# Weight casts queued behind the norm of the first token block, and a latent transposed one unit later

## Chip, cores and metric

One core of a Trainium2 chip. The metric is the device time of one execution in microseconds; of several runs the median counts.

## The reference, cut to what matters

The kernel computes one block of an encoder: x of 256 tokens by 2048 features goes through a gated FFN, a mixer (latent attention beside gated linear attention) and a second gated FFN, each behind a norm with scale and shift.

```python
mod = (jax.nn.silu(c) @ w_ada[i] + b_ada[i]).reshape(B, N_MOD, D)
h = _rms_norm(x, g_ffn1[i]) * (1.0 + sc1) + sh1
x = x + 0.5 * ga1 * _swiglu(h, w1_a[i], w3_a[i], w2_a[i])
h = _rms_norm(x, g_mix[i]) * (1.0 + sc2) + sh2
(q_lat, kv_lat, k_rope_raw, gq, gk, gv, g_lr, g_out, gate_a, gate_b) = _split_cols(h @ w_in[i], IN_SPLITS)
...
x = x + ga2 * (merged @ w_out[i])
h = _rms_norm(x, g_ffn2[i]) * (1.0 + sc3) + sh3
x = x + 0.5 * ga3 * _swiglu(h, w1_b[i], w3_b[i], w2_b[i])
```

The change touches the second and the third `_rms_norm` with the first weights that follow each, and the norm of `kv_lat`.

## The kernel before

**Tiling.** The 256 tokens are two blocks (tb 0 and 1) of 128. x lies in `x_sb`, tokens on partitions. For a product the activations are transposed to `hT` (features on partitions, 16 tiles k of 128), and the weights stream in as units of 1 MB (four k tiles by 512 columns) into one of three `raw` buffers.

**Three products for one.** Each fp32 operand is split in a high part (a cast to fp32r) and a low part (the value less the high part). `split_raw` makes two pieces of 1024 columns of each unit: ScalarE (ACT) casts raw to `wh` (L125), VectorE (DVE) subtracts to `wl` (L126). Six buffers each hold them. `mm3` issues three matmuls, L137 (wh), L140 (wl) and L141 (low activations).

**The end of a stage.** `add_product` makes the last 512 columns (n = 3) in two halves: block 0's matmuls of the last three units first, then `mid`, then block 1's. `mid` calls `resid` for block 0: DVE scales (L405) and adds to x_sb (L407), ACT squares with a sum (L291), `finish_rstd` forms the variance on DVE (L307) and GpSimd (POOL) raises it to -0.5 (L309). Then `then(tb)` from `next_hT` makes hT of the next stage in four groups of four k tiles: `xn_T` scales on ACT (L341) and transposes on PE (L344); `mod_T` applies scale and shift, half on DVE (L356) and half on ACT (L359), casts the high part on ACT (L364) and subtracts the low part on DVE (L365). Block 1 goes the same way after its own matmuls.

**After it.** In the mixer the first product is the kv latent, `lat` (four units, block 0 first for the first three); in the second FFN it is `a1`. After `lat`, `latent` normalizes it (L787 on ACT, L793 `ln` on DVE) and returns `finish`, called `kv_done`, which transposes `ln` on PE (L804), scales (L809) and splits it to ckvh and ckvl (L695, L696). Eight units of `w_qc` follow, in two accumulators, `qc0` and `qc1`, one for each block; `qc1` takes the buffer of `lat`. ckv is first used in `mla_pair(0)`, after the eight units.

**The order.** The kernel is written in program order, and a scheduler puts the instructions on each engine when the program is built: of those that it takes to be ready, the one written first goes first; `high_priority` lifts a block, `keep_in_program_order` pins an instruction. On the chip each engine then goes through its list in that order and waits where an operand or buffer is not there. `issue_after(ins)` adds an edge in this order alone: the instructions of its block on the engine of `ins` are queued behind `ins`. SyncE (SP) issues the weight loads, in order, each as a raw buffer comes free.

Of the kernel before, what the change touches and what calls it, by code (L numbers as in the profile page):

```python
# [10 lines left out]
F32 = mybir.dt.float32  # L11
# [3 lines left out]
ALU = mybir.AluOpType  # L15
# [4 lines left out]
D = 2048  # L20
# [43 lines left out]
def layer_kernel(ctx: ExitStack, tc: tile.TileContext, a: dict):  # L64
    nc = tc.nc
    PE, ACT, DVE, POOL, SP = nc.tensor, nc.scalar, nc.vector, nc.gpsimd, nc.sync
# [45 lines left out]

    last_cast = [None]

    def split_raw(raw, src_cols, n):

        res = []
        per = max(1, (src_cols // n) // 2)
        k = 0
        while k * n < src_cols:  # L120
            w = min(per * n, src_cols - k * n)
            wh = hl.tile([P, 1024], F32R, tag="wh", name="wh")
            wl = hl.tile([P, 1024], F32R, tag="wl", name="wl")
            src = raw[:, k * n:k * n + w]
            last_cast[0] = ACT.copy(wh[:, :w], src)  # L125
            DVE.tensor_tensor(wl[:, :w], src, wh[:, :w].bitcast(F32), op=ALU.subtract)  # L126
            for q in range(w // n):
                res.append((wh[:, q * n:(q + 1) * n], wl[:, q * n:(q + 1) * n]))
            k += w // n
        return res  # L130

    def unit_parts(ap, nkt, n):

        return split_raw(load_unit(ap, nkt * n), nkt * n, n)

    def mm3(out, xh, xl, wh, wl, start, stop, pin=False):
        m = PE.matmul(out, xh, wh, start=start, stop=False)  # L137
        if pin:
            tc.keep_in_program_order(m)
        PE.matmul(out, xh, wl, start=False, stop=False)  # L140
        PE.matmul(out, xl, wh, start=False, stop=stop)  # L141
# [142 lines left out]
    ss_t = const.tile([P, TB, 4], F32, name="ss_t")  # L284
# [11 lines left out]
    def early_rstd():  # L296
# [3 lines left out]
        DVE.tensor_scalar(t[:, TB:2 * TB], t[:, 0:TB], scalar1=1.0 / D, scalar2=EPS, op0=ALU.mult, op1=ALU.add)  # L300
        return POOL.tensor_tensor(rs_t, t[:, TB:2 * TB], mhalf[:, 0:TB], op=ALU.pow)

    def finish_rstd(tb):
        t = wk.tile([P, 16], F32, tag="st", name="ssum", bufs=4)
        DVE.tensor_reduce(t[:, 0:1], ss_t[:, tb, 0:3], axis=AX.X, op=ALU.add)
        DVE.tensor_scalar(t[:, 1:2], t[:, 0:1], scalar1=1.0 / D, scalar2=EPS, op0=ALU.mult, op1=ALU.add)
        DVE.tensor_scalar(t[:, 2:3], ss_t[:, tb, 3:4], scalar1=1.0 / D, scalar2=t[:, 1:2],  # L307
                          op0=ALU.mult, op1=ALU.add)
        POOL.tensor_tensor(rs_t[:, tb:tb + 1], t[:, 2:3], mhalf[:, 0:1], op=ALU.pow)  # L309

    def new_hT_tb(tb):
        return (hTp.tile([P, KT, P], F32R, tag=f"hTh{tb}", name="hTh"),
                hTp.tile([P, KT, P], F32R, tag=f"hTl{tb}", name="hTl"))

    def next_hT(i):

        hT = []

        def then(tb):
            hT.append(new_hT_tb(tb))  # L320
            for kg in range(4):
                with tc.high_priority() if kg == 0 else nullcontext():
                    norm_T(hT, i, tb, kg * 4, 4)
        return hT, then

    def new_hT():
# [5 lines left out]
    def norm_T(hT, i, tb, k0, nk):  # L332

        mod_T(hT, i, tb, k0, nk, xn_T(tb, k0, nk))

    last_xn = [None]

    def xn_T(tb, k0, nk, in_order=False):
        w = nk * P
        xn = wkA("xn")  # L340
        last_xn[0] = ACT.mul(xn[:, :w], x_sb[:, tb, k0 * P:k0 * P + w], rs_t[:, tb:tb + 1])  # L341
        ps = bank("xT")
        for k in range(nk):
            t = PE.transpose(ps[:, k * P:(k + 1) * P], xn[:, k * P:(k + 1) * P], ident)  # L344
            if in_order:
                tc.keep_in_program_order(t)
        return ps

    def mod_T(hT, i, tb, k0, nk, ps, early=False):
        w = nk * P  # L350
        hf = wkB("hf")
        for k in range(nk):
            kt = k0 + k
            o, s_ = hf[:, k * P:(k + 1) * P], ps[:, k * P:(k + 1) * P]
            if k % 2 == 0 and not early:
                DVE.tensor_scalar(o, s_, scalar1=ab[i][:, kt:kt + 1],  # L356
                                  scalar2=ab[i][:, KT + kt:KT + kt + 1], op0=ALU.mult, op1=ALU.add)
            else:
                ACT.activation(o, s_, AF.Identity, scale=ab[i][:, kt:kt + 1],  # L359
                               bias=ab[i][:, KT + kt:KT + kt + 1])  # L360
        hi = hT[tb][0][:, k0:k0 + nk, :]
        lo = hT[tb][1][:, k0:k0 + nk, :]
        hv = hf[:, :w].rearrange("p (k t) -> p k t", k=nk)
        ACT.copy(hi, hv)  # L364
        DVE.tensor_tensor(lo, hv, hi.bitcast(F32), op=ALU.subtract)  # L365
# [34 lines left out]
    def resid_ops(acc, g, n, tbs, tail):  # L400
        nt = len(tbs)
        t = wkA("res")
        tv = t[:, :nt * 512].rearrange("p (t n) -> p t n", t=nt)
        av = acc[tbs[0]].unsqueeze(1) if nt == 1 else acc
        DVE.tensor_tensor(tv, av, g(n).unsqueeze(1).broadcast_to([P, nt, 512]), op=ALU.mult)  # L405
        xv = x_sb[:, tbs[0]:tbs[0] + nt, n * 512:(n + 1) * 512]
        DVE.tensor_tensor(xv, xv, tv, op=ALU.add)  # L407
        for tb in tbs if tail else ():
            sumsq_chunk(tb, n)
            if n == 3:  # L410
                finish_rstd(tb)
# [45 lines left out]
    with tc.tile_pool(name="f1", bufs=1, reuse_waits="tile") as f1, \  # L457
# [185 lines left out]
        for r, grp in enumerate(raws_of):  # L643
            known = set(ada_done)
            fill(int(target(r)) - (n_all - len(ada_q)))
            if r == 0:
                h_tiles(known)
            raw = load_unit(a["w_open"][r], pool=lambda: ramp_raw(True if grp[0][0] == 0 else None))
            if grp[0][0] == 0:
                weights = [raw[:, q * 512:(q + 1) * 512] for q in range(4)]  # L650
            else:
                if grp[0][0] == 1 and len(pacc) < 4:
                    pacc.append([bank("pacc2"), bank("pacc3")])
                    free_slots.insert(0, 3)
                weights = split_raw(raw, 2048, 512)
                do_todo(r)
            if r == 3:
                high_tiles(0, 1, hfs[0])
            low_tiles()
            h_tiles(known)  # L660
            assert not h_rows or all(k < h_rows[0][0] for _, _, _, k in grp), (r, grp, h_rows)
            if any(k0 <= k < k0 + n for k0, n, _ in lows for _, _, _, k in grp):
                low_tiles()
            for q, ((gi, c, wi, k), w) in enumerate(zip(grp, weights)):
                product(r, gi, (c, wi), k, w)
                if gi == 0 and x_blocks and q < 3:
                    with tc.issue_after(first_hf[0].ins):
                        x_blocks.pop(0)()
            if not h_rows and x_again and r >= X_AGAIN:
                x_again.pop(0)()  # L670
            if grp[-1][0] == last_group and (c, wi) not in FRONT[-1] and 3 in free_slots:
                free_slots.remove(3)
# [3 lines left out]
        with tc.issue_after(last_cast[0].ins):  # L676
# [7 lines left out]
        gTs, flush = ffn_up(a["w1_a"], a["w3_a"], chunks, f1r, xs)  # L684
        mod_cols(1, 0, 16, C_GMX)
        hT, then = next_hT(1)
        ffn_down(a["w2_a"], list(chunks), gTs, flush, g_row, True, after=lambda n: fill(1000 if n == 2 else 0),
                 then=then)
# [19 lines left out]
    with tc.tile_pool(name="mx", bufs=1, reuse_waits="tile") as mx:  # L708
# [4 lines left out]
        with tc.tile_pool(name="mla", bufs=1, reuse_waits="tile") as ml:  # L713
# [6 lines left out]
            for tb in range(TB):  # L720
                DVE.tensor_scalar(ang[:, tb * 32:(tb + 1) * 32], rows[:, 128:160],
                                  scalar1=posf[:, tb:tb + 1], scalar2=None, op0=ALU.mult)
# [96 lines left out]

            accs = [acc_tile("qc0"), acc_tile("qc1")]  # L820
            for u in range(8):
                if u == 2:
                    kv_done()
                for j, (wh, wl) in enumerate(unit_parts(a["w_qc"][u], 2, 592)):
                    k = u * 2 + j
                    for tb in range(TB):
                        xh, xl = xs(k, tb)
                        for e, (c0, c1) in enumerate(((0, 320), (320, 592))):
                            mm3(accs[tb][:, e, :c1 - c0], xh, xl, wh[:, c0:c1], wl[:, c0:c1],
                                start=(k == 0), stop=(k == KT - 1))  # L830
# [25 lines left out]
            for tb in range(TB):  # L856
                DVE.tensor_scalar(kr[:, tb, 0, :], accs[tb][:, 0, 256:320], scalar1=krs[:, tb:tb + 1],
                                  scalar2=None, op0=ALU.mult)
# [157 lines left out]
        with tc.tile_pool(name="late", bufs=1, reuse_waits="tile") as lt, ExitStack() as ctx2:  # L1016
# [5 lines left out]
            with tc.tile_pool(name="gla", bufs=1, reuse_waits="tile") as gl:  # L1022
# [11 lines left out]
                for tb in range(TB):  # L1034
# [7 lines left out]
                                             op0=ALU.min, op1=ALU.add)  # L1042
# [156 lines left out]
            lt2 = ctx2.enter_context(tc.tile_pool(name="late2", bufs=1, reuse_waits="tile"))  # L1199
            g_row = gate_rows(lt2, 1, 1.0, "ga2")  # L1200
            hT, then = next_hT(2)
            for n in range(4):
                if n == 3:
# [220 lines left out]
```

## Time and profile before

| | |
|---|---|
| median of 3 runs | 2139.95 us (2137.03 to 2147.26) |
| profiled execution | 2140.67 us, span 2138.8 us |
| PE busy | 2111.7 us (99%) |
| DVE busy | 1626.9 us (76%) |
| ACT busy | 1037.4 us (49%) |
| POOL busy | 41.7 us (2%) |
| the mixer's norm | about 760 to 790 us |
| the kv latent's norm and transposes | about 796 to 809 us |
| the second FFN's norm | about 1396 to 1426 us |

A timeline row gives the start, the duration, engine, line, operation, the tiles written and read, the shape, the count, and in brackets how long the engine was idle before it and what ended that. Ends of matmuls are modelled, so pauses of PE are read from the distance of starts.

### The profile page before, as it was taken

To read this page: it belongs to the slowest core of one execution; us is meant where nothing else is said; L and a number is where in the kernel's file an instruction comes from. 1 tells how busy PE (TensorE), PEld (TensorE's weight loads), DVE (VectorE), ACT (ScalarE), POOL (GpSimd) and SP (SyncE) were. 2 spreads that over 40 slices of the span, in tenths; PEclk is the share of its full clock that TensorE was granted. 3 is DMA by queue.
4 is the path that set the end of the run, shared out by engine and by line. 5 is a ranking of instruction groups with operands and counts; after the bars stand their busy time and mean duration, and the time that the engine had idled before them with its cause. 6 is when DMAs were issued, how large, how long until landed. Compare 5 with 4: busy or idle time off the path is not lost.

```text
span 2138.8 us, 26030 instructions
## 1 busy us (share of the span) xinstructions
PE 2111.7 (99%) x10192; PEld 1759.5 (82%) x10192; DVE 1626.9 (76%) x1840; ACT 1037.4 (49%) x1290; POOL 41.7 (2%) x63
## 2 busy tenths in 40 slices
PE   8999999999999999999999999999999999999998
PEld 6678888888888879888878788778888888888886
DVE  6898768887787877665777788887688678857875
ACT  6445433334343455655544434475455445535553
POOL 0000000000000001010000000000000000000000
PEclk9999999999999999999999999999999999999999
DMA  9999668998998846445878788955555545555563
GB/s 374 346 382 340 236 243 326 345 347 332 325 339 320 322 145 224 154 170 202 297 290 295 285 337 314 323 200 197 206 188 194 207 174 195 212 197 197 177 216 119
DMA packets 78670, 550.30 MB, mean 257 GB/s; under 512 B 9361, under 2 KB 9921, under 8 KB 13266
## 3 DMA queue, kind: packets, MB, share of 16 engines
q1 hardware_dynamic: 75744, 542.06, 69.3%
q0 software_dynamic: 1344, 3.17, 0.7%
q10 hardware_dynamic: 1458, 3.40, 0.5%
q8 instruction: 80, 1.31, 0.2%
q14 instruction: 44, 0.36, 0.0%
HBM read 546.47 MB, written 2.12 MB: 256 GB/s over the span
## 4 chain that ended last, share of the span: by engine, by line
PE 87%; DVE 5%; DMA 4%; ACT 2%; issue 1%; POOL 0%; SPq 0%; POOLq 0%; ACTq 0%
PE a L137 9%; PE a L141 9%; PE a L140 9%; PE y L137 8%; PE y L140 8%; PE y L141 8%; PE pacc L140 2%; PE pacc L141 2%; PE pacc L137 2%; DVE wl L126 2%; DMA raw<-in_w_open 2%; DMA raw<-in_w_out 2%; PE qkv L137 1%; DVE raw L194 1%; PE gb L137 1%; PE ga L141 1%
## 5 line engine op out<-in xcount | busy, mean ns | idle before, releaser
L125 ACT CAST wh<-raw 128x1024 fp32r<-128x1024 f32 (+2 forms) x678 | 690.3, 1040 | 871.7 <-DMA raw<-in_w_a 217.4
L126 DVE TENSOR_TENSOR wl<-raw,wh 128x1024 fp32r<-128x1024 f32 (+2 forms) x678 | 804.6, 1208 | 339.0 <-ACT wh L125 336.7
L194 DVE SCALAR_TENSOR_TENSOR raw<-raw,c_bc 128x2048 f32<-128x2048 f32 x144 | 329.0, 2286 | 24.4 <-DMA raw<-in_w_ada 23.2
L137 PE MATMUL a<-wh,hTh 128*128 128x512 f32 (+1 forms) x904 | 340.1, 376 | 0.1
L140 PE MATMUL a<-wl,hTh 128*128 128x512 f32 (+1 forms) x904 | 339.5, 376 | 0.0
L141 PE MATMUL a<-wh,hTl 128*128 128x512 f32 (+1 forms) x904 | 339.3, 375 | 0.0
L137 PE MATMUL y<-wh,gT 128*128 128x512 f32 x704 | 275.8, 392 | 0.2
L140 PE MATMUL y<-wl,gT 128*128 128x512 f32 x704 | 274.1, 389 | 0.0
L141 PE MATMUL y<-wh,gT 128*128 128x512 f32 x704 | 273.7, 389 | 0.0
L141 PEld LDWEIGHTS a<-wh,hTl 128*128 128x128 f32 x904 | 170.2, 188 | 31.0 <-DVE hTl L365 0.3
L137 PEld LDWEIGHTS a<-wh,hTh 128*128 128x128 f32 x904 | 170.3, 188 | 30.3 <-ACT wh L125 0.6
L140 PEld LDWEIGHTS a<-wl,hTh 128*128 128x128 f32 x904 | 170.4, 188 | 29.2
L137 PEld LDWEIGHTS y<-wh,gT 128*128 128x128 f32 x704 | 132.2, 188 | 29.6 <-ACT gT L388 1.8
L141 PEld LDWEIGHTS y<-wh,gT 128*128 128x128 f32 x704 | 132.2, 188 | 27.6 <-DVE gT L389 0.2
L140 PEld LDWEIGHTS y<-wl,gT 128*128 128x128 f32 x704 | 132.2, 188 | 26.9
L140 PE MATMUL pacc<-wl,hTh 128*128 128x512 f32 x360 | 142.6, 396 | 4.3 <-DVE wl L126 4.2
L141 PE MATMUL pacc<-wh,hTl 128*128 128x512 f32 x360 | 141.6, 393 | 0.7 <-DVE hTl L547 0.7
L137 PE MATMUL pacc<-wh,hTh 128*128 128x512 f32 x360 | 137.7, 396 | 3.8 <-ACT wh L125 3.0
L1256 DVE TENSOR_TENSOR wl<-right,wh 128x1024 fp32r<-128x1024 f32 x60 | 73.5, 1224 | 30.3 <-ACT wh L1255 29.7
L1255 ACT CAST wh<-right 128x1024 fp32r<-128x1024 f32 x60 | 63.2, 1053 | 55.7 <-PE m L141 24.5
L140 PEld LDWEIGHTS pacc<-wl,hTh 128*128 128x128 f32 x360 | 68.3, 190 | 21.8 <-DVE wl L126 7.5
L137 PEld LDWEIGHTS pacc<-wh,hTh 128*128 128x128 f32 x360 | 68.2, 189 | 19.9 <-ACT wh L125 4.3
(350 smaller groups left out, 3095.3 us busy)
## 6 DMA issues: line engine op xcount, KB each, us to landing
raw<-in_w_ada SPq DMA_DIRECT2D x144, 1024.0 KB, 5.9
raw<-in_w_b SPq DMA_DIRECT2D x102, 1024.0 KB, 4.8
raw<-in_w_a SPq DMA_DIRECT2D x84, 1024.0 KB, 5.6
raw<-in_w_in SPq DMA_DIRECT2D x60, 1024.0 KB, 5.1
raw<-in_w_open SPq DMA_DIRECT2D x48, 1024.0 KB, 6.4
raw<-in_w_s SPq DMA_DIRECT2D x30, 1024.0 KB, 4.9
raw<-in_w_out SPq DMA_DIRECT2D x16, 1024.0 KB, 6.5
raw<-in_w_proj_a SPq DMA_DIRECT2D x8, 1024.0 KB, 4.7
```

What stands on the lines that cost most here:

```text
L125: last_cast[0] = ACT.copy(wh[:, :w], src)
L126: DVE.tensor_tensor(wl[:, :w], src, wh[:, :w].bitcast(F32), op=ALU.subtract)
L137: m = PE.matmul(out, xh, wh, start=start, stop=False)
L140: PE.matmul(out, xh, wl, start=False, stop=False)
L141: PE.matmul(out, xl, wh, start=False, stop=stop)
L194: last_ada[0] = DVE.scalar_tensor_tensor(out=raw, in0=raw, scalar=1.0, in1=c_bc, op0=ALU.mult, op1=ALU.mult, accum_out=dst)
L1255: ACT.copy(wh[:, :n], src)
L1256: DVE.tensor_tensor(wl[:, :n], src, wh[:, :n].bitcast(F32), op=ALU.subtract)
```

## The change

Every call of `then(0)` from `next_hT` (there are two, for the mixer and the second FFN) notes two instructions: block 0's first scaling `xn` on ACT and its variance on DVE, twice each. The next two calls of `split_raw` take one such pair each and queue their casts behind the first and their subtracts behind the second. Besides, `kv_done` is called before unit 3 of `w_qc`, not before unit 2.

```diff
+    gates = []
+
     def split_raw(raw, src_cols, n):
...
-            last_cast[0] = ACT.copy(wh[:, :w], src)
-            DVE.tensor_tensor(wl[:, :w], src, wh[:, :w].bitcast(F32), op=ALU.subtract)
+            with tc.issue_after(gates[0][0].ins) if gates else nullcontext():
+                last_cast[0] = ACT.copy(wh[:, :w], src)
+            with tc.issue_after(gates[0][1].ins) if gates else nullcontext():
+                DVE.tensor_tensor(wl[:, :w], src, wh[:, :w].bitcast(F32), op=ALU.subtract)
             for q in range(w // n):
                 res.append((wh[:, q * n:(q + 1) * n], wl[:, q * n:(q + 1) * n]))
             k += w // n
+        if gates:
+            gates.pop(0)
         return res
...
+    last_var = [None]
+
     def finish_rstd(tb):
...
-        DVE.tensor_scalar(t[:, 2:3], ss_t[:, tb, 3:4], scalar1=1.0 / D, scalar2=t[:, 1:2],
-                          op0=ALU.mult, op1=ALU.add)
+        var = DVE.tensor_scalar(t[:, 2:3], ss_t[:, tb, 3:4], scalar1=1.0 / D, scalar2=t[:, 1:2],
+                                op0=ALU.mult, op1=ALU.add)
         POOL.tensor_tensor(rs_t[:, tb:tb + 1], t[:, 2:3], mhalf[:, 0:1], op=ALU.pow)
+        last_var[0] = var
...
             for kg in range(4):
                 with tc.high_priority() if kg == 0 else nullcontext():
                     norm_T(hT, i, tb, kg * 4, 4)
+                if tb == 0 and kg == 0:
+                    gates.extend([(last_xn[0], last_var[0])] * 2)
         return hT, then
...
             for u in range(8):
-                if u == 2:
+                if u == 3:
                     kv_done()
```

## Rows read from the trace of the kernel before

**Rows 1.** The page, share of busy time by engine.
```profile
PE 2111.7 (99%) x10192; PEld 1759.5 (82%) x10192; DVE 1626.9 (76%) x1840; ACT 1037.4 (49%) x1290; POOL 41.7 (2%) x63
```

**Rows 2.** Busy time by stretch: from:to, us, each engine's busy us, PEclk, DMA, GB/s.
```profile
756.00:795.00 39.00, 37.70 (x178) 29.79 (x176) 30.43 (x72) 27.30 (x49) 1.87 (x4) 1.00 0.37 117
795.00:835.00 40.00, 39.16 (x257) 36.82 (x256) 31.07 (x82) 21.34 (x39) 2.10 (x3) 1.00 0.59 210
...
1392.00:1432.00 40.00, 38.67 (x181) 30.46 (x180) 33.09 (x59) 30.04 (x51) 1.12 (x2) 1.00 0.50 190
```

**Rows 3.** The chain of waits at the mixer's norm: start, us, what.
```profile
761.51 0.85 issue
...
800.72 0.42 PE qc L137
```

**Rows 4.** Timeline of PE at the mixer's norm.
```profile
764.15 0.39 PE L140 MATMUL y<-wl,gT 128*128 128x512 f32 x1
764.38 0.39 PE L141 MATMUL y<-wh,gT 128*128 128x512 f32 x1
765.36 0.66 PE L344 MATMUL xT<-small,xn 128*128 128x128 f32 x4 [0.60 <-ACT xn L341]
...
774.99 0.39 PE L140 MATMUL lat<-wl,hTh 128*128 128x512 f32 x1
...
776.05 0.66 PE L344 MATMUL xT<-small,xn 128*128 128x128 f32 x4 [0.22 <-ACT xn L341]
```

**Rows 5.** Timeline of ACT at the mixer's norm.
```profile
761.40 1.05 ACT L125 CAST wh<-raw 128x1024 fp32r<-128x1024 f32 x1 [8.46 <-PE y L141]
762.36 0.63 ACT L291 ACTIVATE junk<-x_sb 128x512 f32<-128x512 f32 x1
762.89 0.19 ACT L291 ACTIVATION_READ_ACCUMULATOR junk<-x_sb 128x1 f32 x1
...
765.83 1.03 ACT L125 CAST wh<-raw 128x1024 fp32r<-128x1024 f32 x1
...
770.41 2.95 ACT L125 CAST wh<-raw 128x1024 fp32r<-128x1024 f32 x3
...
784.20 1.04 ACT L125 CAST wh<-raw 128x1024 fp32r<-128x1024 f32 x1
```

**Rows 6.** Timeline of DVE at the mixer's norm.
```profile
760.77 0.69 DVE L407 TENSOR_TENSOR x_sb<-x_sb,res 128x512 f32<-128x512 f32 x1
762.49 1.23 DVE L126 TENSOR_TENSOR wl<-raw,wh 128x1024 fp32r<-128x1024 f32 x1 [1.03 <-ACT wh L125]
763.63 0.21 DVE L307 TENSOR_SCALAR ssum<-ss_t,ssum 128x1 f32<-128x1 f32 x1
764.05 1.22 DVE L126 TENSOR_TENSOR wl<-raw,wh 128x1024 fp32r<-128x1024 f32 x1 [0.21 <-ACT wh L125]
...
773.21 1.22 DVE L126 TENSOR_TENSOR wl<-raw,wh 128x1024 fp32r<-128x1024 f32 x1
```

**Rows 7.** Timeline of POOL at the mixer's norm.
```profile
763.99 0.56 POOL L309 TENSOR_TENSOR rs_t<-ssum,mhalf 128x1 f32<-128x1 f32 x1 [354.10 <-DVE ssum L307]
```

**Rows 8.** Timeline of PE at the second FFN's norm.
```profile
1401.57 0.66 PE L344 MATMUL xT<-small,xn 128*128 128x128 f32 x4 [0.54 <-ACT xn L341]
```

**Rows 9.** Timelines at the kv latent: PE, then DVE, then PE.
```profile
799.26 0.29 PE L141 MATMUL qc<-wh,hTl 128*128 128x272 f32 x1
799.96 0.33 PE L804 MATMUL lat_ps<-small,ln 128*128 128x128 f32 x1 [0.41 <-DVE ln L793]
800.72 0.42 PE L137 MATMUL qc<-wh,hTh 128*128 128x320 f32 x1 [0.43 <-DVE ln L793]
...
807.97 0.68 DVE L696 TENSOR_TENSOR ckvl<-lf,ckvh 128x512 fp32r<-128x512 f32 x1
...
824.37 0.40 PE L137 MATMUL ka<-wh,ckvh 128*128 128x512 f32 x1
```

**Rows 10.** The page, DMA issues: count, KB each, median us to landing.
```profile
raw<-in_w_in SPq DMA_DIRECT2D x60, 1024.0 KB, 5.1
```

## Prediction

> **What bounds the kernel now.** I read the page's share of busy time first: TensorE (PE) is busy for 99% of the span [rows 1]. So the time can fall only where PE pauses, and the windows show how little that is at the places of the change: the granted clock is 1.00 (the 2.4 GHz level) in all three, and PE is idle for 39.00 - 37.70 = 1.30 us around the mixer's norm, 40.00 - 39.16 = 0.84 us around the kv latent and 40.00 - 38.67 = 1.33 us around the second FFN's norm [rows 2]. Together 3.47 us. A matmul's row lasts 0.39 us while starts in a run lie 0.23 us apart [rows 4], so each pause hides up to 0.16 us more; I counted a dozen pauses in the PE timelines of these windows, some 1.9 us. No more than 3.47 + 1.9 = 5.4 us (0.25%) can be won, all of it together.
>
> Then the chain of waits. It leaves PE when the last residual of block 0 is added, spends 0.85 us in "issue" (an engine that waits for nothing it needs), goes through ScalarE (ACT), VectorE (DVE) and GpSimd (POOL), and is back on PE for good only at 800.72 [rows 3]. The 0.85 us is what the change aims at. x_sb is complete at 760.77 + 0.69 = 761.46 [rows 6]; its square could start then, but ACT began a weight cast of 1.05 us at 761.40 and the square starts at 762.36 [rows 5]: 0.86 us late. The sum of squares is read out by 762.89 + 0.19 = 763.08 [rows 5]; DVE could form the variance at about 763.15, but a weight subtract of 1.23 us holds it from 762.49, and it starts at 763.63 [rows 6]: 0.48 us late. The norm chain of block 0 is therefore 0.86 + 0.48 = 1.34 us late, and PE, standing before the transposes of xn, pauses from 764.38 + 0.23 = 764.61 to 765.36 [rows 4]: 0.75 us. The second FFN has the same order of work and a pause of 0.54 us idle [rows 8] and the hidden 0.16, 0.70 us.
>
> **The change part by part.** The gates add and remove no instruction. The two casts and two subtracts of each of the next two units (four pieces of 1024 columns) get an issue order: casts behind the first xn on ACT, subtracts behind the variance on DVE. Of the four casts, only the first two run ahead of xn today (761.40 and the second one between the read-out and xn); the third starts at 765.83 and the fourth in the group of three at 770.41, both behind xn already [rows 5]. So the gates move two casts and two subtracts for each norm, nothing more. An issue order is no wait: no engine stands still for a new semaphore. What is queued behind the held casts on ACT is later casts; on DVE later subtracts.
>
> What the chain gains is 1.34 us, for both norms (the second has the same rows).
>
> What the move costs: the gap in which the first two subtracts ran (762.49 to 765.27, [rows 6]) goes empty on DVE. One of the four now takes the hole that the third has today, behind 765.83; two more than today then stand behind block 0's hTl, where only the fourth stands now, at 773.21 [rows 6]. Each occupies DVE for 1.14 us: the next instruction starts at 763.63 behind the subtract of 762.49 [rows 6]. At least piece 2 has to go before block 1's residual: PE needs it 7 matmuls into lat. So block 1's chain, which starts with that residual on DVE, is 1.34 - 1.14 = 0.2 us earlier, not 1.34. PE meets block 1's chain again at its transposes at 776.05, where it waits today too [rows 4]; whatever PE wins at 765.36 and the second chain doesn't, it loses there. **I take 0.2 us for each norm**, 0.4 together. From above: if the residual goes first, the full pause, 0.75 + 0.70 = 1.45 us, and at best all idle time. From below: two more subtracts than today put piece 4's end at 773.21 + 1.22 - 1.34 + 2 x 1.14 = 775.37; PE wants it at 774.99 [rows 4], so it would wait 0.38 us. For two norms that is 0.76 us lost.
>
> DMA: a held subtract frees its raw buffer later. With three buffers the load of lat's fourth unit can go out when the second subtract ends, at 764.05 + 1.22 = 765.27 [rows 6]; held, at about 771.2. A transfer of 1 MB takes 5.1 us [rows 10], so it lands at about 776.3, and its cast starts at 784.20 [rows 5]: 7.9 us of cover. The loads behind it on SP's queue wait for pieces 3 and 4 anyway. I cost it at nothing; without that cover it would be 771.2 - 765.27 = 5.9 us for each norm.
>
> The kv latent: `kv_done` issues 8 transposes, 8 scalings, 2 casts and 2 subtracts, no DMA. All are written one unit later, behind the matmuls of unit 2. Today PE ends the qc matmuls of block 0 at 799.26 + 0.13 = 799.39, waits for ln until 799.96 (0.57 us), does one transpose of about 0.09 us, and waits until 800.72 for the second ln [rows 9], which also frees the accumulator that the qc matmuls of block 1 want. With the transposes written later, unit 2's matmuls of block 0 may stand in their place: their first weight piece is ready. The second wait stays if block 1's matmuls are then put next. So the bounds are 0.1 us lost (the order is the same and one transpose no longer fills a hole) and 800.72 - 799.39 - 0.09 = 1.24 us won; I take the first wait, **0.57 us**, since only the transposes cause that one. Later work is covered: the last ckvl subtract starts at 807.97 and ckv is first used at 824.37 [rows 9], 15.7 us apart against a shift of one unit, 24 matmuls of 0.13 to 0.15 us, 3.3 us.
>
> Sum: 0.2 + 0.2 + 0.57 = 1.0 us. The profiled execution took 2140.67 us (span 2138.8 and 1.87 around it), 0.72 above the median of the runs, 2139.95; taken off the profiled one it gives 2139.7, off the median **2139.0**, which I forecast.
>
> A rule that speaks against the change: in the rows, the GpSimd power that makes rstd starts at 763.99 and lasts 0.56 us although a subtract starts on DVE at 764.05 [rows 6, 7]; the one that started first was not held up. The Trainium skill, "SBUF — State Buffer", "Who interferes with whom", says that a VectorE instruction with two SBUF inputs contends with a GpSimd one that reads SBUF, and that the second to issue blocks fully. That row agrees as far as it goes; no row has the other order. For block 0 the other order can't arise: a gated subtract needs its cast, the cast stands behind xn, and xn waits for the power. For block 1 it can, and that is a rival below.
>
> **The rivals.**
> (a) The gate moves the transposes too. PE's order is also made when the program is built, by the same scheduler; if it sees xn 1.34 us earlier it may put the transposes six matmuls earlier, and PE pauses there as before. For it: a hand-over that the pause at 765.36 shows to be longer than planned. The change then doesn't do what it says: 0, 2140.0.
> (b) The second chain gets its gain as well: block 1's residual, squares and power are not behind the extra subtracts. Then the pauses of both norms mostly go: 2 x 1.3 us of idle and 0.84 at the latent, up to 5.4 with the hidden parts; the middle is 2136.5. Against it: DVE has little free time there, 30.43 busy of 39 us [rows 2].
> (c) Slower: piece 4 comes late at both norms, by 0.38 us each, with nothing won at the latent: 2139.95 + 0.76 = 2140.7. It decides from the point where two subtracts stand between block 0's hTl and block 1's variance.
> (d) Slower: more subtracts are left when block 1's variance is formed, one of them is queued directly behind it, and the power has to wait for it. Today tensor_scalars from PSUM stand there. Price: a subtract of 1.22 us less the 0.2 us that the hand-over to POOL takes anyway, 1.0 us on block 1's chain for each norm: 2142.0.
>
> **How the numbers follow.** The forecast 0.48; (a) 0.20; (b) 0.14; (c) 0.12; (d) 0.04; 0.02 for an order that changes in a way I can't price. The range: below, all that can be won, 2139.95 - 5.4 = 2134.5; above, (c) and (d) together with the latent's 0.1, 2139.95 + 0.76 + 2.0 + 0.1 = 2142.8, and 1 us for the runs, of which the lowest and the highest of before lie 10 us apart: 2143.8. 0.5% is 10.7 us, about what a measurement of this kernel can tell from no change; all pauses together are half of it. So faster by more than that 0.01, the same 0.97, slower 0.02.
>
> **What would show it.** In the changed profile, the first xn of each norm about 1.3 us closer behind x_sb; no cast between x_sb and xn on ACT; PE's pause before the first xT gone or short. The step from 1.34 to 0.2 is right if block 1's res starts no more than a few tenths earlier relative to lat's first matmul, and wrong if the pause before its xT shrinks too. At the latent, qc matmuls stand at the end of unit 1's where the lone transpose stood. The prediction is wrong if PE waits for wh or wl in the first units of lat or a, if a cast waits for DMA there, or if the order changes away from these places.

## The result and the profile after

The changed kernel takes 2147.49 us (median of 21 runs, 2142.03 to 2152.57), the kernel before beside it 2142.04 us (21 runs): a ratio of 1.0025 with an interval of 1.0017 to 1.0033, that is 5.4 us slower (3.6 to 7.1). The difference is within 0.5%, as forecast, but on the other side, and the time lies above the range. Of the miss of 8.5 us against the forecast, 2.1 is the reference: more runs put the kernel before at 2142.04 and not at 2139.95.

The profiled execution of the changed kernel took 2142.66 us, span 2140.9 us, one of its fastest. The page's first line hardly differs from [rows 1]; GpSimd has 3 us more:

```profile
PE 2111.0 (99%) x10192; PEld 1759.0 (82%) x10192; DVE 1627.2 (76%) x1840; ACT 1039.4 (49%) x1290; POOL 44.7 (2%) x63
```

The windows of [rows 2], after (the same columns; behind the five engines stands the granted clock, 1.00 or 0.96):

```profile
756.00:795.00 39.00, 35.67 (x170) 28.35 (x169) 29.34 (x69) 27.55 (x49) 3.32 (x4) 1.00 0.32 106
795.00:835.00 40.00, 38.89 (x257) 36.71 (x256) 31.79 (x83) 21.37 (x40) 2.10 (x3) 1.00 0.62 211
...
1392.00:1432.00 40.00, 36.80 (x170) 29.34 (x169) 30.20 (x53) 29.29 (x49) 2.63 (x2) 0.96 0.46 166
```

PE is idle for 3.33 and 3.20 us at the two norms, against 1.30 and 1.33. POOL is busy for 3.32 and not 1.87 us, and for 2.63 and not 1.12. At the second FFN the mean granted clock is 0.96. In the latent's window PE is idle for 0.27 us more.

Now the mixer's norm engine by engine, after. ACT first (compare [rows 5]):

```profile
760.55 0.63 ACT L297 ACTIVATE junk<-x_sb 128x512 f32<-128x512 f32 x1 [8.61 <-DVE x_sb L418]
761.09 0.19 ACT L297 ACTIVATION_READ_ACCUMULATOR junk<-x_sb 128x1 f32 x1
762.27 1.33 ACT L352 ACTIVATE xn<-x_sb,rs_t 128x512 f32<-128x512 f32 x2 [0.99 <-POOL rs_t L317]
...
776.18 0.72 ACT L352 ACTIVATE xn<-x_sb,rs_t 128x512 f32<-128x512 f32 x1 [1.68 <-POOL rs_t L317]
```

Block 0's chain is as quick as it was meant to be: no cast stands between x_sb and the square, and xn starts 0.99 us behind the end of the read-out, 0.56 of it the power. Block 1's xn, the last row, waits 1.68 us for POOL. Then DVE and POOL (compare [rows 6, 7]):

```profile
768.91 0.73 DVE L367 TENSOR_SCALAR hf<-xT,ab 128x128 f32<-128x128 f32 x2
769.55 1.21 DVE L130 TENSOR_TENSOR wl<-raw,wh 128x1024 fp32r<-128x1024 f32 x1
770.69 0.69 DVE L416 TENSOR_TENSOR res<-y,ga 128x512 f32<-128x512 f32 x1
...
771.61 0.68 DVE L418 TENSOR_TENSOR x_sb<-x_sb,res 128x512 f32<-128x512 f32 x1
...
772.66 1.22 DVE L130 TENSOR_TENSOR wl<-raw,wh 128x1024 fp32r<-128x1024 f32 x1
773.80 0.21 DVE L315 TENSOR_SCALAR ssum<-ss_t,ssum 128x1 f32<-128x1 f32 x1
773.92 1.22 DVE L130 TENSOR_TENSOR wl<-raw,wh 128x1024 fp32r<-128x1024 f32 x1
775.06 0.68 DVE L376 TENSOR_TENSOR hTl<-hf,hTh 128x512 fp32r<-128x512 f32 x1
...
761.67 0.56 POOL L317 TENSOR_TENSOR rs_t<-ssum,mhalf 128x1 f32<-128x1 f32 x1 [351.91 <-DVE ssum L315]
774.15 2.00 POOL L317 TENSOR_TENSOR rs_t<-ssum,mhalf 128x1 f32<-128x1 f32 x1 [11.09 <-DVE ssum L315]
```

Block 1's variance ends at about 774.0. A weight subtract follows right behind it at 773.92, then hTl. The power on one column takes 2.00 us instead of 0.54 and ends at 776.15, 0.41 us after hTl. In the kernel before, two scalings stood behind that variance, whose input xT lies in a PSUM bank and not in SBUF. The power was over in 0.54 us there:

```profile
774.34 0.21 DVE L307 TENSOR_SCALAR ssum<-ss_t,ssum 128x1 f32<-128x1 f32 x1
774.47 0.72 DVE L356 TENSOR_SCALAR hf<-xT,ab 128x128 f32<-128x128 f32 x2
774.69 0.54 POOL L309 TENSOR_TENSOR rs_t<-ssum,mhalf 128x1 f32<-128x1 f32 x1 [9.31 <-DVE ssum L307]
```

And PE, after (compare [rows 4]):

```profile
763.04 0.66 PE L355 MATMUL xT<-small,xn 128*128 128x128 f32 x4 [0.64 <-ACT xn L352]
...
773.94 0.50 PE L146 MATMUL lat<-wl,hTh 128*128 128x512 f32 x1 [1.10 <-DVE wl L130]
...
776.96 0.66 PE L355 MATMUL xT<-small,xn 128*128 128x128 f32 x4 [1.59 <-ACT xn L352]
```

The pause before the first transposes, which the change was to take away, is still there (0.64 us, 0.60 before). Two longer ones are new: 1.10 us for the low half of the third weight piece, whose subtract (772.66) now stands behind the residual, and 1.59 us for block 1's xn, 0.22 before.

### The profile page after: what moved, and what is told of

It is laid out like the page before. It is cut to its first block, busy times and chain, and to the rows that moved or that the text cites. A ratio compares the mean times of both kernels' runs of the same rounds, so it can differ in the third digit from the quotient of the medians.

```text
span 2140.9 us, 26035 instructions
## 1 busy us (share of the span) xinstructions
PE 2111.0 (99%) x10192; PEld 1759.0 (82%) x10192; DVE 1627.2 (76%) x1840; ACT 1039.4 (49%) x1290; POOL 44.7 (2%) x63
## 4 chain that ended last, share of the span: by engine, by line
PE 90%; DVE 4%; DMA 3%; ACT 2%; issue 1%; POOL 0%; SPq 0%; POOLq 0%; ACTq 0%
PE a L143 9%; PE a L146 9%; PE a L147 9%; PE y L143 9%; PE y L146 9%; PE y L147 9%; DMA raw<-in_w_open 2%; PE pacc L146 2%; PE pacc L147 2%; PE pacc L143 2%; DVE wl L130 2%; PE qkv L143 1%; PE gb L143 1%; PE ga L147 1%; PE qkv L146 1%; PE ga L143 1%
```

## The experiments

Each ratio but the changed kernel's compares 11 or 12 runs with runs of the kernel before on the same chip. The sums of PE's waits are those of the view of waits, PE alone, at each norm. A row of that view reads: who waited for whom, us in total, times, longest. For the changed kernel it has, at the mixer's norm and then at the second FFN's:

```profile
PE xT L355 <- ACT xn L352: 2.2, 2, 1.6
PE lat L146 <- DVE wl L130: 1.1, 1, 1.1
...
PE xT L355 <- ACT xn L352: 2.2, 2, 1.6
PE a L146 <- DVE wl L130: 1.0, 1, 1.0
```

The path is what PE's stream loses in all: from the start of block 0's residual to the first `qc` matmul at the mixer's norm, and to the 145th `a` matmul at the second FFN's (by then the transposes are past), less the same in the kernel before. A star marks a norm behind which the granted clock fell.

| kernel | PE waits, mixer + FFN (us) | against before | path against before, mixer, FFN | ratio, interval |
|---|---|---|---|---|
| before | 1.2 + 1.2 | | | |
| changed | 3.3 + 3.2 | +4.1 | +1.7, +2.8* | 1.0025 (1.0017 to 1.0033) |
| changed, second execution | 3.3 + 3.2 | +4.1 | +3.1*, +1.5 | one execution |
| gates only | 3.3 + 3.2 | +4.1 | +1.7, +1.5 | 1.0025 (1.0014 to 1.0036) |
| latent only | 1.2 + 1.4 | +0.2 | 0.0, 0.0 | 0.9997 (0.9986 to 1.0007) |
| fourth subtract behind the power | 1.7 + 2.3 | +1.6 | +0.9, +0.4 | 1.0005 (0.9994 to 1.0016) |
| casts behind the square | 1.9 + 1.6 | +1.1 | +0.3, +0.1 | 1.0000 (0.9989 to 1.0012) |
| both cures | 0.4 + 0.7 | -1.3 | -0.2, -0.8 | 0.9991 (0.9981 to 1.0001) |
| both cures, again | 0.5 + 0.7 | -1.2 | -0.2, -0.7 | 0.9995 (0.9982 to 1.0007) |
| and left sums behind the power | 0.5 + 0.6 | -1.3 | -0.3, +0.1 | 0.9995 (0.9984 to 1.0007) |
| gates at the mixer only | 3.3 + 1.6 | +2.5 | +2.7*, +0.3 | 1.0006 (0.9994 to 1.0019) |
| gates at the second FFN only | 1.2 + 3.2 | +2.0 | 0.0, +3.0* | 1.0009 (0.9996 to 1.0021) |

**Which part.** The gates alone, from the changed kernel:

```diff
-                if u == 3:
+                if u == 2:
                     kv_done()
```

> The changed kernel with kv_done back before unit 2: the gates alone. Theory (all of the loss is in block 1's norm chain, behind the gates): as slow as the changed kernel, 5 us over before, and in the profile block 1's power on GpSimd 2.0 us long in both norms. Rival (the moved latent carries part of it): clearly less, 2 to 4 us over before.

Measured: 1.0025, power 2.00 and 2.07 us, PE's waits as in the changed kernel. The latent alone, from the kernel before:

```diff
-                if u == 2:
+                if u == 3:
                     kv_done()
```

> The kernel before with kv_done before unit 3: the latent alone. Theory: no difference, within 0.5 us, because the wait for the second ln, which frees the accumulator of block 1, stays and grows by what the lone transpose filled. My forecast's step: 0.6 us faster. Rival: 1 us and more slower, because ckv comes 3.3 us later.

Measured: 0.9997. So the whole loss is the gates', and the latent's step brings nothing that can be measured. Its PE rows (compare [rows 9]):

```profile
801.32 0.31 PE L137 MATMUL qc<-wh,hTh 128*128 128x320 f32 x1
802.65 0.41 PE L137 MATMUL qc<-wh,hTh 128*128 128x320 f32 x1 [1.02 <-DVE ln L793]
```

One matmul of unit 2 stands where the lone transpose stood, and then PE waits for the second ln in one piece, 1.02 us, where it waited twice before, 0.41 and 0.43 us. From the first qc matmul to the first `ka` matmul it is 826.26 - 798.07 = 28.19 us, and was 824.37 - 796.13 = 28.24.

**The held power.** One wait more in the changed kernel:

```diff
...
-                DVE.tensor_tensor(wl[:, :w], src, wh[:, :w].bitcast(F32), op=ALU.subtract)
+                low = DVE.tensor_tensor(wl[:, :w], src, wh[:, :w].bitcast(F32), op=ALU.subtract)
+            if len(gates) == 1 and k:
+                tc.add_manual_dep(low.ins, last_pow[0].ins.name, ...)
...
-        POOL.tensor_tensor(rs_t[:, tb:tb + 1], t[:, 2:3], mhalf[:, 0:1], op=ALU.pow)
+        last_pow[0] = POOL.tensor_tensor(rs_t[:, tb:tb + 1], t[:, 2:3], mhalf[:, 0:1], op=ALU.pow)
```

> The changed kernel with one wait more: the second subtract of the second gated unit (the one that stands right behind block 1's variance) waits for block 1's power. VectorE stands still for some 0.7 us, and nothing else is different. Theory (the subtract holds the power up): the power takes 0.56 us again, xn of block 1 comes 1.4 us earlier, PE's pause before block 1's first transposes falls from 1.8 to about 0.4 us in each norm, the granted clock stays at 1.00 after the second norm, and the time is 0 to 2 us over before. Rival (the backlog of subtracts is the cause, and PE would wait for weights anyway): PE's pauses add up to the same, the time stays 4 to 5 us over before.

DVE and POOL at the mixer's norm of this kernel, and at the second FFN's:

```profile
774.91 0.21 DVE L320 TENSOR_SCALAR ssum<-ss_t,ssum 128x1 f32<-128x1 f32 x1
775.85 1.23 DVE L131 TENSOR_TENSOR wl<-raw,wh 128x1024 fp32r<-128x1024 f32 x1 [0.72 <-POOL rs_t L322]
...
775.27 0.55 POOL L322 TENSOR_TENSOR rs_t<-ssum,mhalf 128x1 f32<-128x1 f32 x1 [11.09 <-DVE ssum L320]
...
1411.30 0.68 DVE L1238 TENSOR_TENSOR left<-hTh,hTl 128x512 f32<-128x512 f32 x1
1412.05 0.69 DVE L381 TENSOR_TENSOR hTl<-hf,hTh 128x512 fp32r<-128x512 f32 x1
...
1411.46 0.93 POOL L322 TENSOR_TENSOR rs_t<-ssum,mhalf 128x1 f32<-128x1 f32 x1 [11.71 <-DVE ssum L320]
```

VectorE now stands still for 0.72 us, and the kernel is faster than the changed one for it: 1.0005. The power is back at 0.55 us in the mixer. In the second FFN it is 0.93: there a sum of `left_sums` with two operands in SBUF, 0.68 us long, moved up behind the variance. Three lengths, then, by what stands behind: 0.55 us (nothing, or scalings from PSUM), 0.93 (0.68 us of two-operand work), 2.00 (1.22 and 0.68 in a row; 2.07 in the second FFN). The rival, that the backlog is the cause and the pauses add up to the same, falls.

**The late subtract.** The casts queued behind block 0's last square and not behind xn, from the changed kernel:

```diff
...
+            last_sq[0] = ACT.activation(j[:, :512], xv, AF.Square, accum_out=acc)
...
+            sq = last_sq[0]
...
-                    gates.extend([(last_xn[0], last_var[0])] * 2)
+                    gates.extend([(sq, last_var[0])] * 2)
```

> The changed kernel with the casts queued behind block 0's last square and not behind its first xn, so that they may fill the 1 us in which ScalarE waits for the power. Theory (two causes, a late subtract for PE and a held power): PE's wait for the low half of the third piece, 1.3 us now, is gone, the power of block 1 is still held by the subtract behind the variance; about 2 to 3 us over before. Rival (the backlog alone): as fast as before or faster. Rival (the held power alone): 4 to 5 us over before.

```profile
776.54 0.50 PE L147 MATMUL lat<-wl,hTh 128*128 128x512 f32 x1 [0.25 <-DVE wl L131]
779.56 0.66 PE L357 MATMUL xT<-small,xn 128*128 128x128 f32 x4 [1.57 <-ACT xn L354]
...
776.75 1.99 POOL L318 TENSOR_TENSOR rs_t<-ssum,mhalf 128x1 f32<-128x1 f32 x1 [11.11 <-DVE ssum L316]
```

One cast fits into the 1 us in which ACT waits for the power, its subtract into the hole on DVE; the third piece comes almost in time (0.25 us), and the pause before block 0's transposes is gone from the view. The power is held as before, and PE waits 1.57 us for it. I had expected 2 to 3 us over before; it is 1.0000, and by the path 0.3 and 0.1 us over: the first block's gain, which the expectation left out, pays for the held power.

**Both.** The casts behind the square, and the third unit's subtracts behind the power:

```diff
...
+            if third[0] == 1:
+                tc.add_manual_dep(low.ins, last_pow[0].ins.name, ...)
...
+        third[0] -= 1
...
-                    gates.extend([(last_xn[0], last_var[0])] * 2)
+                    gates.extend([(sq, last_var[0])] * 2)
+                    third[0] = 3
```

> Both cures in one: the casts queued behind block 0's last square, and the subtracts of the third unit, the first of which stands right behind block 1's variance, wait for block 1's power. Theory (two separate causes, each seen alone): no wait for a weight subtract over 0.5 us, power 0.55 us in the mixer and at most 0.9 in the second FFN (there another VectorE instruction with two operands in SBUF stands behind it), PE's pauses in both norms 2 to 3 us less than before's, the time 0 to 3 us under before. Rival (what the first block wins is always lost at the second): the same as before within 1 us.

Measured: 0.9991, interval 0.9981 to 1.0001, and a second time:

> The kernel with both cures once more, for a narrower interval. Theory: 1 to 2.5 us under before, by the pauses of its first profile 1 us and by a clock that stays at 1.00 behind both norms no more. Rival: no difference, the first result was chance.

0.9995, 0.9982 to 1.0007. Against the changed kernel (1.0025) this is clearly faster. Against the kernel before each interval reaches 1; by the path both profiles pass the two norms 1.0 us sooner, so a gain of about 1 us is likely, and the times don't show it. PE's waits fell by 1.3 us, not by the 2 to 3 that I had expected. The rest of the held power in the second FFN was taken away too:

```diff
...
-                DVE.tensor_tensor(f[:, tb], hi, lo, op=ALU.add)
+                left = DVE.tensor_tensor(f[:, tb], hi, lo, op=ALU.add)
+                if kg == 0:
+                    tc.add_manual_dep(left.ins, last_pow[0].ins.name, ...)
```

> As the kernel with both cures, and in the second FFN the first two sums of left_sums (two operands in SBUF, the first of them stood right behind block 1's variance) wait for block 1's power too. Theory: that power takes 0.55 us and not 0.93, PE's pauses there fall by 0.3 to 0.5 us, the time is 2 to 3 us under before. Rival: the pauses only move, as fast as the kernel with both cures.

```profile
1410.41 0.55 POOL L325 TENSOR_TENSOR rs_t<-ssum,mhalf 128x1 f32<-128x1 f32 x1 [11.73 <-DVE ssum L323]
```

The power is 0.55 us, but other small waits came in its place (0.4 us for a cast, 0.2 for hTh): 0.9995, nothing more gained, and the path at this norm went from -0.8 back to +0.1. Here the rival was right.

**What the waits leave over.** PE's waits rise by 4.1 us, but not all of that is lost: some of the kernel before's time at the norms goes in pauses that the view of waits doesn't list. The path counts both. Its two ends at the mixer's norm, in the kernel before and then in the changed one:

```profile
760.04 0.69 DVE L405 TENSOR_TENSOR res<-y,ga 128x512 f32<-128x512 f32 x1 [5.85 <-PE y L141]
796.13 0.30 PE L137 MATMUL qc<-wh,hTh 128*128 128x320 f32 x1
...
759.04 0.69 DVE L416 TENSOR_TENSOR res<-y,ga 128x512 f32<-128x512 f32 x1 [5.85 <-PE y L147]
796.83 0.30 PE L143 MATMUL qc<-wh,hTh 128*128 128x320 f32 x1
```

That is 36.09 and 37.79 us, 1.7 lost. At the second FFN's norm it is 47.08 us before and 48.61 in the gates alone, 1.5 lost. So the pauses cost 1.7 + 1.5 = 3.2 us, less than the 5.4 measured and under its interval (3.6 to 7.1). The changed kernel once more, one execution:

> The changed kernel once more, for a second profile. Theory: PE's pauses in both norms are those of the first profile within 0.3 us, since the order is fixed; where the granted clock falls may be elsewhere, and the difference between the two executions is what it costs.

It took 2147.57 us, with the same waits (3.3 + 3.2). The 4.9 us between the two executions are not what a fall of the clock costs, as I had thought: block 0's residual at the mixer's norm starts at 759.04 us in the one and at 764.13 in the other, so they arise ahead of the first norm that the change touches. The windows of this execution at the mixer's norm, and then those of the first profile at the second FFN's:

```profile
776.00:780.00 4.00, 2.91 (x13) 2.12 (x12) 4.00 (x9) 3.60 (x7) 0.75 (x1) 1.00 0.77 262
780.00:784.00 4.00, 2.40 (x9) 1.67 (x9) 2.30 (x5) 2.72 (x5) 1.24 (x1) 0.78 0.48 152
784.00:788.00 4.00, 4.00 (x21) 3.56 (x20) 3.47 (x8) 3.16 (x6) 0.00 (x0) 0.79 0.00 0
...
1408.00:1412.00 4.00, 2.88 (x12) 1.72 (x10) 4.00 (x7) 3.12 (x7) 1.44 (x1) 1.00 0.75 262
1412.00:1416.00 4.00, 2.57 (x9) 2.17 (x10) 2.29 (x4) 3.21 (x5) 0.62 (x1) 0.60 0.74 262
```

In the second of the two pauses or just behind it the granted clock falls, here to 0.69 from 1412 to 1414 and to 0.50, the lower of the two levels (1.2 GHz), from 1414 to 1416, and PE's rows show it:

```profile
1413.43 1.12 PE L355 MATMUL xT<-small,xn 128*128 128x128 f32 x4 [1.58 <-ACT xn L352]
1414.20 0.78 PE L143 MATMUL a<-wh,hTh 128*128 128x512 f32 x1
1414.77 0.63 PE L146 MATMUL a<-wl,hTh 128*128 128x512 f32 x1
1415.20 0.63 PE L147 MATMUL a<-wh,hTl 128*128 128x512 f32 x1
```

Starts are 0.43 us apart and not 0.23. The path at this norm is 48.60 us in the execution in which the clock stayed up and 49.84 in the one in which it fell, and at the mixer's norm 37.79 and 39.14: 1.2 to 1.4 us for such a fall. Next the gates were set for one norm only:

```diff
-                if tb == 0 and kg == 0:
+                if tb == 0 and kg == 0 and i == 1:
```

> The changed kernel with gates for the mixer alone. If the loss is the sum of the pauses, 1.7 us of the 3.2 are here: 1.7 us over before. If a part of it comes from the clock after the second FFN's pauses, less than half of the 5.4 us is here: 1 to 2 us over before, and the granted clock after both norms is 1.00.

and with `i == 2`:

> The changed kernel with gates for the second FFN alone. By the pauses 1.5 us over before; with the clock's part 3 to 4 us over before, and the granted clock under 1.00 behind the norm in this profile or not, since it is not so in every execution.

Both are between (1.0006 and 1.0009); the intervals are too wide to say how much each norm has of the loss. I had expected the clock to stay at 1.00 behind the mixer's norm; each of the two profiles shows the fall behind its gated norm, 0.67 and 0.73 in one window of 4 us, and 1.00 behind the other one:

```profile
778.00:782.00 4.00, 2.43 (x10) 1.80 (x9) 2.30 (x5) 2.60 (x5) 1.23 (x1) 0.67 0.49 154
...
1420.00:1424.00 4.00, 4.00 (x18) 3.19 (x17) 3.41 (x6) 3.85 (x7) 0.00 (x0) 0.73 0.26 107
```

Over all profiles, a norm with both long pauses was passed eight times (twice each in the changed kernel, its second execution and the gates alone, once each in the two above), and the clock fell behind four of them. A norm with at most one such pause was passed sixteen times, four of them with just one, and it fell behind none. But two pauses of that size are not needed: in the gates alone it fell once more, at the end of the stage before the second FFN's norm, where no gate is, behind pauses of 1.34 and 0.53 us for a late weight:

```profile
1382.89 0.73 PE L143 MATMUL y<-wh,hTh 128*128 128x512 f32 x2 [1.34 <-ACT wh L128]
1384.15 0.50 PE L146 MATMUL y<-wl,hTh 128*128 128x512 f32 x1 [0.53 <-DVE wl L130]
...
1384.00:1388.00 4.00, 3.85 (x11) 3.04 (x12) 4.00 (x5) 2.40 (x3) 1.09 (x2) 0.62 0.26 58
```

Half of two falls at 1.3 us each is 1.3, and 3.2 + 1.3 = 4.5 us, inside the measured interval and below its middle. That the clock carries the rest is consistent with this and not shown: eight passages are few, and an experiment that keeps PE at work through the pauses was not made.

## Why the prediction was wrong

**The lateness of block 0's chain: right.** From the end of x_sb to xn it took 764.59 - 761.46 = 3.13 us, now 762.27 - 760.46 = 1.81: 1.32 us less, against 1.34 forecast.

**PE's first pause: rival (a).** The transposes were put earlier by as much as the chain, so the pause stayed (0.64 us idle). Between block 0's residual and the transposes PE has six matmuls fewer, as (a) says. The casts behind the square, in whose order the scheduler put matmuls differently, made the pause go.

**The step that failed: "block 1's chain, which starts with that residual on DVE, is 1.34 - 1.14 = 0.2 us earlier".** From it came the gain of 0.2 us for each norm; by the path each norm lost, 1.7 and 1.5 us. I counted one subtract of 1.14 us behind block 0's hTl and stopped there. From the end of block 0's x_sb to block 1's residual it took 9.77 us and now 10.23: 0.46 us more, not 0.2 less, since two scalings (768.91) came along with the subtract (769.55) in front of the residual. And I took what follows the residual as it was. There (d) happened, to which I gave 0.04: the subtracts that were left included one right behind the variance. I had the mechanism and the place, but took the order behind the variance as given, although the change pushes two subtracts towards just that place; with 1.14 us each on an engine with 8.6 us free in 39, a subtract ready at that point was to be expected. Its price was mis-sized too: 1.0 us forecast, 2.00 - 0.54 = 1.46 measured, because hTl followed the subtract without a gap and the power was let in only behind both.

**The weights: (c) happened as well.** Not piece 4 by 0.38 us but piece 3 by 1.10 us: the residual is lifted by `high_priority`, so the third subtract came behind residual and sum, not ahead of them. I had let piece 3 pass as on time. PE waiting for wl in the first units of lat and a is also what the prediction named as a sign of being wrong.

**They came together.** (c) and (d) stood as two cases of 0.12 and 0.04, with the sum of both only in the range's end. One cause, two subtracts pushed back, makes both at once. Their prices in the range, 0.76 + 2.0, were to be 2 x 1.1 + 2 x 1.4 = 5.0 by the waits measured, of which the path leaves 3.2.

**The clock** was in no term; the table of windows gave 1.00 everywhere before, and I took it to stay. A fall cost 1.2 to 1.4 us in the rows above.

**The latent** came near the lower bound: unit 2 gave one matmul, then block 1's accumulator was waited for, 0 instead of 0.57 us. Without the fall of the clock the sum over the terms would have been a loss of 3.2 us, and not a gain of 1.0.

**DMA: right.** No cast waits for a load at the mixer's norm after the change, and ckv is there in time.

The Trainium skill, "SBUF — State Buffer", "Who interferes with whom", says that the second to issue of a VectorE instruction with two SBUF inputs and a GpSimd one that reads SBUF blocks fully. The runs agree where a two-operand instruction was first: the power took 0.93 and 2.00 us. Scalings from PSUM did not hold it (0.54 in the kernel before). The other direction is not shown: in the kernel before a subtract starts at 764.05, 0.06 us into the power's row, and its own row is 1.22 us long [rows 6, 7], as elsewhere. So the prediction's "That row agrees as far as it goes" holds for the power, which was first and was not held, and not for the subtract, which was second and shows no block either.

## What to carry to other kernels

When work is queued behind a chain to make room for it, look at what the pushed work will stand in front of next: here two subtracts moved from a hole into the next block's chain and cost more there. Queue filler behind the first instruction that truly needs the engine (the square), not behind the last of the chain (xn): the chain's own waits are the holes for it. A tiny GpSimd power on a critical chain was quick here only where the next VectorE instruction was one without two SBUF operands, or came later; a wait of 0.7 us on VectorE bought 1.4 us of the power and 0.8 us of PE's path. An order edge moves more than the instructions it names: the transposes went forward with the chain, and PE's first pause stayed.

## What was not expected of the hardware

A held GpSimd instruction is not let in between two VectorE instructions that follow each other closely: its row starts at 774.15, the subtract ends at 775.14, hTl runs from 775.06 to 775.74, and the power ends at 776.15, 0.41 us behind hTl. A gap of 0.07 us was enough: with the fourth subtract behind the power, at the second FFN's norm, the add to `left` ends at 1411.98, hTl starts at 1412.05, and the power ends at 1412.39, 0.41 us behind the add, while hTl still runs. The power's row counts the blocked time as its own, so the page shows a busy POOL, 44.7 against 41.7 us, and no wait.

A pause of 1.1 us and then one of 1.6 us were followed by the lower clock in four passages of eight, one of them alone in none of four, and two shorter ones at another place, 1.34 and 0.53 us, once. Two executions with the same order and the same waits at the norms took 2142.66 and 2147.57 us; the difference arose in the stages before.
